# Ten steps of block 2's modulation a layer move from block 1's MLP to its attention

## The chip, the core and the metric

The kernel runs on one core of one Trainium2 chip. A core has five engines, each with its own queue of instructions, worked off in order: PE (TensorE, matrix products), DVE (VectorE) and ACT (ScalarE) for elementwise work, POOL (GpSimd), and SP (SyncE), which here only issues DMA transfers. The engines wait for one another through semaphores. The metric is the device time of one execution in microseconds (us); the profile and the trace come from one such execution, in which a hardware profiler took down each instruction's start and duration. In the rows PE is TensorE's matmuls and PEld its loads of the stationary operand; L12 is line 12 of the kernel.

## The reference, cut to what matters

Two blocks of two layers each, on 256 tokens of width 1024, in float32. Block 1's layer is attention of three kinds, then attention to a memory, then an MLP; each is followed by a layer norm. Block 2's layer needs the vector `mod`, which depends on the input `c` alone, and so can be worked out at any time before.

```python
def first_block(x, mem, ...):
    for l in range(DEPTH):                                   # DEPTH = 2
        y = hybrid_mixer(x, w_in[l], ..., w_gate[l], w_br_nsa[l], w_br_mla[l], w_br_fox[l], w_mix_out[l])
        x = layer_norm(DN_ALPHA * x + y, ln_g[l, 0], ln_b[l, 0])
        y = memory_cross_attention(x, mem, xa_w_q[l], xa_w_kv[l], xa_w_o[l])
        x = layer_norm(DN_ALPHA * x + y, ln_g[l, 1], ln_b[l, 1])
        y = jnp.square(jax.nn.relu(x @ mlp_w_up[l])) @ mlp_w_down[l]     # 1024 x 4096, 4096 x 1024
        x = layer_norm(DN_ALPHA * x + y, ln_g[l, 2], ln_b[l, 2])
    return x

def hybrid_layer(x, c_act, ...):                             # block 2, c_act = silu(c)
    mod = c_act @ w_ada + b_ada                              # w_ada is 1024 x 3072
    shift, scale, gate = jnp.split(mod[:, None, :], 3, axis=-1)
    h = rms_norm_2(x, norm_g) * (1.0 + scale) + shift
    ...
    return x + gate * (merged @ w_out)
```

## The kernel before

Every matrix product is made of three: each float32 operand is split in a rounded part hi and a rest lo, and `mm3` (L138 to L140) issues hi x hi, hi x lo and lo x hi. Weights come in pieces of 128 x 1024 numbers (512 KB). `raw_load` has SP fetch one into the tile `raw` (L76, four buffers); ACT casts it to `hi` (L112), DVE subtracts to get `lo` (L113); `hi` and `lo` have six buffers each. So a buffer of `raw` comes free when DVE has made `lo`, and only then can SP issue the next load: SP's queue is worked off in order, and a load that waits for a buffer holds up those behind it.

**The modulation.** `mod` of a layer is made by 24 steps (`ada_steps`). Each loads 512 KB of `w_ada` into a buffer of `raw` and has DVE multiply it with the conditioning vector and sum along each row (L1641: one instruction of 128 x 1024 and a short one that reads the sum). Neither ACT nor PE takes part. The first step of a layer also loads `c` into `raw`, takes its Tanh on ACT (L1637) and makes silu's double on DVE (L1638) into a tile of the tag `gt`. The steps stand in the list `fillers`, and `fill(n)` runs the next n of it.

**Where they run.** The MLP of block 1 calls `fill`. `up(g)` makes a quarter of the hidden layer: 8 pieces of `w_up`, four PSUM banks `s` one after the other, each cleared by ACT's Relu (L921) and Square (L925), POOL's square (L926) and DVE's difference (L927); behind each bank of `up(1)` to `up(3)` stands a `fill(1)`, twelve in a layer. `down(g)` takes 8 pieces of `w_down`, in two halves; behind each half of `down(0)` and `down(1)` stands a `fill(2)`, and of `down(2)` a `fill(4)`, sixteen in a layer. The order is up 0, up 1, down 0, up 2, down 1, up 3, down 2, down 3. In layer 0 the list begins with `clear_scratch` (POOL clears a tile of the tag `flat` and writes it to two scratch arrays in DRAM, L1660), in layer 1 with the three steps of `trig_steps`.

**What sets the order.** A scheduler orders ACT, DVE, POOL and SP by data, buffers and priorities; in the attention of block 1 PE's order is written by hand (`manual_schedule`): 22 slots, each a piece of two attention jobs, and behind each slot a piece of the dense products (`w_in`'s last parts, then the gates, `w_gate`). The scores of a head block are read by DVE (L275), exponentiated by ACT (L279), scaled by DVE (L286, L288, L290), transposed by PE (L302) and copied from PSUM by ACT (L313) or DVE (L315) in turn. The one bank `t` serves these transposes and those of the compressed attention (L627), so L627 must wait until L315 has copied the bank. L677 takes the copied scores to the values. After the attention to the memory the normalized tokens are transposed by PE (L357) and cast by ACT and DVE (L127, L128); beside that `up_by_token` has made the first 512 hidden features by token (L894 Relu, L895 square on POOL), and `by_feature` transposes them (L902).

Of the kernel before, what the change touches and what calls it, by code (L numbers as in the profile page):

```python
# [42 lines left out]
def program(ctx: ExitStack, tc: tile.TileContext, T: dict, out: bass.AP):  # L43
# [21 lines left out]
    def bt(tag, shape, dt=F32, bufs=1):  # L65
        p = com if tag in COMMON else blk[0]
        return p.tile(shape, dt, tag=tag, name=nm(tag), bufs={**COMMON, "dg": 2, "TT": 2, "Tn": 2}.get(tag, bufs))
# [126 lines left out]
    fillers = []  # L194
# [200 lines left out]
    def block1_layer(l, x, xop, us, K):  # L395
# [10 lines left out]
        if not K:  # L406
            r = [flat2(bt("P", [128, 4, 256], F32, 4)) for g in range(2)]
            w, (h, lo) = raw_tile(), slots()
            for k in range(2):
                x_tiles(0, r[0], k, k + 1)  # L410
                c = slice(512 * k, 512 * k + 512)
# [28 lines left out]
        for j in range(0, 4, 2):  # L440
            p = pst("mm")
# [14 lines left out]
        pool.memset(rep, 0.0)  # L456

        def compress_hidden(i):
            fl = bt("flat", [128, 16, 2, 16])
            pool.memset(fl[:, :, :, 15:16], 0.0)  # L460
            for g in range(2):
                for par in range(2):
                    a = kvT[64 * g:64 * g + 64, i, :]
                    srcv = bass.AP(tensor=a.tensor, offset=a.offset + par,
                                   ap=[list(a.ap[0]), [2, 16], [16, 15]])
                    ver.tensor_add(out=fl[64 * par:64 * par + 64, :, g, 0:15], in0=srcv,
                                   in1=pe_c[64 * g:64 * g + 64, i, par, :].unsqueeze(2).broadcast_to([64, 16, 15]))
            hp = pst("t")
            for kt in range(16):
                q = 32 * (kt % 4)  # L470
                pe.matmul(hp[q:q + 32, :128], lhsT=fl[:, kt].rearrange("p g c -> p (g c)"),
                          rhs=cw1[i][kt // 8][:, 128 * (kt % 8):128 * (kt % 8) + 128], start=kt < 4, stop=kt > 11)
            hq = flat2(bt("PT", [128, 4, 128], F32, 4))[:, 0:128]
            act.copy(out=hq, in_=hp[:, :128])
            hp = pst("t")
            pe.matmul(hp[:, :32], lhsT=hq, rhs=fold4, start=True, stop=True)
            hx = st("hx", [128, 32])
            act.copy(out=hx, in_=hp[:, :32])
            u = st("hu", [128, 32])
            ver.tensor_mul(out=u, in0=hx, in1=hx)  # L480
            ver.tensor_scalar(out=u, in0=u, scalar1=0.044715, scalar2=1.0, op0=ALU.mult, op1=ALU.add)
            ver.tensor_mul(out=u, in0=u, in1=hx)
            act.activation(out=u, in_=u, func=AF.Tanh, scale=math.sqrt(2.0 / math.pi))
            ver.scalar_tensor_tensor(out=hx, in0=u, scalar=1.0, in1=hx, op0=ALU.add, op1=ALU.mult)
            return hx
# [26 lines left out]
        for t in range(2):  # L512
            p = pst("s")
# [210 lines left out]
        with tc.manual_schedule(engines={mybir.EngineType.PE}):  # L724
            if first:
                turn()
            job = {"m": attend_mla, "f": attend_fox, "c": attend_compressed}
            jobs = {}
            pieces = dense()
            for slot in ("m0", "c0", "m1", "m0 c0", "m0 00", "m1 c1", "m1 01", "00 c1", "00 f0", "01 10", "01 10", "f0",  # L730
                         "f0 f1", "10", "10", "10 11", "11", "f1", "f1", "11", "11", "11"):
                for n in slot.split():
                    if n not in jobs:
                        jobs[n] = job[n[0]](int(n[1])) if n[0] in job else attend_nsa(int(n[0]), int(n[1]))
                    next(jobs[n], None)
                next(pieces, None)
            for _ in pieces:
                pass
        x = xs[0]
# [194 lines left out]
        def down(g, op):  # L934
            for c in range(2):
                us = [unit(T["w_down"][l, 16 * c + 4 * g + i]) for i in range(4)]
                gemm_a([ys[0][c], ys[1][c]], op, us, first=g == 0, last=g == 3, t_outer=g == 3 and c == 1)
                if g < 3:
                    fill(2 if g < 2 else 4)
                    continue  # L940
                if c == 1:
                    nrm.params(l, 2)
                    if l + 1 < L:
                        after.extend(unit(T["w_in"][l + 1, 4 + i]) for i in range(4))
                    else:
                        after.append(unit(T["w_wlal"][0], 128, 8))
                        after.append(unit(T["w_in2"][0, 0], 256, 4, pool))
                for t in range(2):
                    nrm.add(t, c, ys[t][c])
                    if c == 1:  # L950
                        nrm.finish(t)
# [662 lines left out]
    def finish(x, r):  # L1614

        fg = aux(T["final_g"].partition_broadcast(128))
        for i in range(2):
            for t in range(2):
# [6 lines left out]
                                         op0=ALU.mult, op1=ALU.mult)  # L1625
                fetch(out[128 * t:128 * t + 128, s], o)

    def ada_steps(l):

        box = {}  # L1630

        def step(j, i):
            def f():
                if not box:
                    r = raw_load(T["c"].partition_broadcast(128))
                    c = box["c"] = bt("gt", [128, 1024])
                    act.activation(out=c, in_=r, func=AF.Tanh, scale=0.5)  # L1637
                    ver.scalar_tensor_tensor(out=c, in0=c, scalar=1.0, in1=r, op0=ALU.add, op1=ALU.mult)  # L1638
                r = raw_load(T["w_ada"][l, j, i])
                o = 8 * j + i  # L1640
                ver.tensor_tensor_reduce(out=r, in0=r, in1=box["c"], scale=1.0, scalar=0.0, op0=ALU.mult,  # L1641
                                         op1=ALU.add, accum_out=mods[l][:, o:o + 1])
                if i == 7:
                    m = mods[l][:, 8 * j:8 * j + 8]
                    ver.scalar_tensor_tensor(out=m, in0=m, scalar=0.5, in1=pv2[l][:, 8 * j:8 * j + 8],
                                             op0=ALU.mult, op1=ALU.add)
                    if j == 1:
                        ver.scalar_tensor_tensor(out=m, in0=m, scalar=1.0, in1=pv2[l][:, 24:32],
                                                 op0=ALU.add, op1=ALU.mult)
            return f  # L1650

        return [step(j, i) for j in range(3) for i in range(8)]
# [1 line left out]
    scratch = {n: dr.tile([128 * 2080], F32, name=n) for n in ("zd", "lt")}  # L1654

    def clear_scratch():
        z = bt("flat", [128, 16, 2, 16]).rearrange("p a b c -> p (a b c)")[:, 0:416]
        pool.memset(z, 0.0)
        for d in scratch.values():
            pool.dma_start(out=flat(d, 0, [2080, 128], [416, 5], [1, 416]),  # L1660
                           in_=z.unsqueeze(1).broadcast_to([128, 5, 416]))
# [45 lines left out]
    with tc.tile_pool(name="b1", bufs=1) as b1, tc.tile_pool(name="s1", bufs=3) as s1:  # L1707
        blk[:] = b1, s1
        xop = new_op(8)
        for l in range(L):  # L1710
            fillers.extend((trig_steps() if l == 1 else [clear_scratch]) + ada_steps(l))
            x, xop, us = block1_layer(l, x, xop, us, K1)
    r = xop
    fill(99)
# [189 lines left out]
```

## Time and profile before

| | |
|---|---|
| median of 3 runs | 1619.14 us (1618.19 to 1619.34) |
| profiled execution | 1620.32 us, of it span 1618.5 us |
| mean granted clock of TensorE over the span | 0.978 of 2.4 GHz |
| PE busy in the span | 1554.8 us, 96% |
| DVE busy | 1100.4 us, 68% |
| ACT busy | 744.8 us, 46% |
| POOL busy | 261.1 us, 16% |

The span runs from the first to the last instruction; what the execution's time has beside it (1.8 us) lies around that. In the trace layer 0 of block 1 has its attention at about 70 to 200 us and its MLP at 290 to 475 us, layer 1 at about 520 to 650 and 745 to 930 us; block 2 follows. A row of the timeline is an instruction's start and duration, its engine and line, the tile it writes and those it reads, and in square brackets how long the engine had been idle before it and whose work ended that.

### The profile page before, as it was taken

How to read it: one execution, taken by the hardware profiler on the slowest of the kernel's cores; microseconds unless marked ns; L12 is line 12 of the kernel's file. 1: busy time of each engine (PE TensorE's matmuls, PEld its weight loads, DVE VectorE, ACT ScalarE, POOL GpSimd, SP SyncE). 2: the span in 40 equal slices, each digit the busy share in tenths (PEclk: the TensorE clock that was granted, in tenths of full speed). 3: DMA queues.
4: the chain of work that ended last, by engine and by line, in shares of the span. 5: the costliest groups of instructions: out<-in, count | busy, mean ns of one | idle time of the engine just before them, and what ended most of it. 6: DMA issues, size and time to landing. Idle time of an engine off the chain costs nothing. (4 is left out here: it accounts for less than half of the span.)

```text
span 1618.5 us, 29835 instructions
## 1 busy us (share of the span) xinstructions
PE 1554.8 (96%) x12106; PEld 1432.2 (88%) x12106; DVE 1100.4 (68%) x1785; ACT 744.8 (46%) x1196; POOL 261.1 (16%) x255
## 2 busy tenths in 40 slices
PE   7999999999999999999999899899999998999998
PEld 6789997999878899988988788899999987999997
DVE  5576568767676766689776787666466775764754
ACT  4665444544445664455543374433444643333441
POOL 1000110101100001201111142401111433201202
PEclk9899999999999999999999989999999999999999
DMA  8733475587776234664777744543355435442451
GB/s 296 257 105 119 158 231 172 179 287 264 266 258 204 89 108 154 204 208 141 253 270 252 265 140 161 162 147 120 102 183 161 155 113 168 163 134 90 154 184 67
DMA packets 81033, 288.98 MB, mean 179 GB/s; under 512 B 9224, under 2 KB 10304, under 8 KB 80896
## 3 DMA queue, kind: packets, MB, share of 16 engines
q1 hardware_dynamic: 78768, 280.07, 51.9%
q0 software_dynamic: 2128, 7.01, 1.5%
q8 instruction: 95, 1.56, 0.4%
q14 instruction: 42, 0.34, 0.1%
HBM read 281.48 MB, written 5.55 MB: 177 GB/s over the span
## 5 line engine op out<-in xcount | busy, mean ns | idle before, releaser
L113 DVE TENSOR_TENSOR lo<-raw,hi 128x1024 fp32r<-128x1024 f32 (+1 forms) x429 | 543.3, 1275 | 227.3 <-ACT hi L112 224.6
L112 ACT CAST hi<-raw 128x1024 fp32r<-128x1024 f32 (+1 forms) x435 | 452.7, 1048 | 508.8 <-PE mm L139 220.9
L138 PE MATMUL mm<-act,hi 128*128 128x256 f32 x1744 | 506.1, 290 | 7.8 <-ACT hi L112 5.8
L140 PE MATMUL mm<-act,lo 128*128 128x256 f32 x1744 | 497.7, 285 | 3.2 <-DVE lo L113 3.2
L139 PE MATMUL mm<-act,hi 128*128 128x256 f32 x1744 | 497.0, 285 | 0.5 <-DVE act L128 0.5
L138 PEld LDWEIGHTS mm<-act,hi 128*128 128x128 f32 x1744 | 336.8, 193 | 15.8 <-ACT hi L112 6.2
L140 PEld LDWEIGHTS mm<-act,lo 128*128 128x128 f32 x1744 | 336.4, 193 | 5.4 <-DVE lo L113 3.9
L139 PEld LDWEIGHTS mm<-act,hi 128*128 128x128 f32 x1744 | 336.6, 193 | 2.0 <-DVE act L128 0.9
L138 PE MATMUL s<-act,hi 128*128 128x256 f32 x448 | 128.5, 287 | 5.5 <-ACT PT L921 5.5
L138 PE MATMUL mm<-hi,act 128*128 128x512 f32 (+1 forms) x320 | 125.2, 392 | 6.5 <-ACT hi L127 5.5
L140 PE MATMUL s<-act,lo 128*128 128x256 f32 x448 | 128.2, 286 | 0.0
L139 PE MATMUL s<-act,hi 128*128 128x256 f32 x448 | 128.2, 286 | 0.0
L139 PE MATMUL mm<-lo,act 128*128 128x512 f32 (+1 forms) x320 | 123.4, 386 | 0.9 <-DVE lo L113 0.9
L140 PE MATMUL mm<-hi,act 128*128 128x512 f32 (+1 forms) x320 | 123.2, 385 | 0.0
L138 PEld LDWEIGHTS s<-act,hi 128*128 128x128 f32 x448 | 87.4, 195 | 6.4 <-ACT PT L921 6.1
L139 PEld LDWEIGHTS s<-act,hi 128*128 128x128 f32 x448 | 87.3, 195 | 0.2
L140 PEld LDWEIGHTS s<-act,lo 128*128 128x128 f32 x448 | 87.5, 195 | 0.0
L1641 DVE CUSTOM_DVE_ANT_0 raw<-raw,gt 128x1024 f32<-128x1024 f32 x48 | 59.5, 1239 | 30.6 <-DMA raw<-in_w_ada 30.3
L138 PEld LDWEIGHTS mm<-hi,act 128*128 128x128 f32 x320 | 61.1, 191 | 19.6 <-ACT hi L127 5.5
L926 POOL TENSOR_TENSOR PT<-PT 128x512 f32<-128x512 f32 x28 | 38.5, 1376 | 236.3 <-ACT act L925 128.4
L138 PE MATMUL mm<-hi,P 128*128 128x512 f32 x192 | 74.8, 389 | 0.0
L139 PE MATMUL mm<-lo,P 128*128 128x512 f32 x192 | 74.8, 389 | 0.0
(519 smaller groups left out, 2439.8 us busy)
## 6 DMA issues: line engine op xcount, KB each, us to landing
raw<-in_w_in SPq DMA_DIRECT2D x119, 512.0 KB, 4.4
raw<-in_w_up SPq DMA_DIRECT2D x64, 512.0 KB, 4.5
raw<-in_w_down SPq DMA_DIRECT2D x64, 512.0 KB, 4.7
raw<-in_w_gate SPq DMA_DIRECT2D x48, 512.0 KB, 3.4
raw<-in_w_ada SPq DMA_DIRECT2D x48, 512.0 KB, 4.5
raw<-in_w_gl SPq DMA_DIRECT2D x48, 512.0 KB, 3.8
raw<-in_w_branch SPq DMA_DIRECT2D x24, 512.0 KB, 3.4
raw<-in_w_br SPq DMA_DIRECT2D x16, 512.0 KB, 3.3
```

The lines of the kernel that those rows point to most:

```text
L112: act.copy(out=h[:, :cols], in_=r[:, :cols])
L113: (eng or ver).tensor_sub(out=l[:, :cols], in0=r[:, :cols], in1=h.bitcast(F32)[:, :cols])
L138: pe.matmul(o, lhsT=lh, rhs=rh, start=first, stop=False)
L139: pe.matmul(o, lhsT=lh, rhs=rl, start=False, stop=False)
L140: pe.matmul(o, lhsT=ll, rhs=rh, start=False, stop=last)
L926: pool.tensor_mul(out=r, in0=r, in1=r)
L1641: ver.tensor_tensor_reduce(out=r, in0=r, in1=box["c"], scale=1.0, scalar=0.0, op0=ALU.mult, op1=ALU.add, accum_out=mods[l][:, o:o + 1])
```

## The change

Nine steps of each layer (the count stops at 20, and 18 of the 22 slots have more than three jobs begun, of which every odd one counts) are run in the attention, by a `fill(1)` behind a slot. What is left of the list runs in the MLP as before, with a `fill(1)` behind each half of `down(0)` to `down(2)`: six there instead of sixteen. `clear_scratch` and `trig_steps` come behind the tenth step. `c` is loaded once, in layer 0's attention, and its product stays in a tile of its own, `cmod`, for both layers; the tiles `flat` become tiles of the tag `mv`.

```diff
         def compress_hidden(i):
-            fl = bt("flat", [128, 16, 2, 16])
+            fl = bt("mv", [128, 16, 2, 16])
...
             pieces = dense()
+            beside = 0
             for slot in ("m0", "c0", "m1", "m0 c0", "m0 00", "m1 c1", "m1 01", "00 c1", "00 f0", "01 10", "01 10", "f0",
                          "f0 f1", "10", "10", "10 11", "11", "f1", "f1", "11", "11", "11"):
                 for n in slot.split():
...
                     next(jobs[n], None)
                 next(pieces, None)
+                if len(jobs) > 3:
+                    beside += 1
+                    if beside % 2 and beside < 20:
+                        fill(1)
...
                 if g < 3:
-                    fill(2 if g < 2 else 4)
+                    fill(1)
                     continue
...
+    box = {}
+
     def ada_steps(l):
 
-        box = {}
 
         def step(j, i):
             def f():
                 if not box:
                     r = raw_load(T["c"].partition_broadcast(128))
-                    c = box["c"] = bt("gt", [128, 1024])
+                    c = box["c"] = bt("cmod", [128, 1024])
                     act.activation(out=c, in_=r, func=AF.Tanh, scale=0.5)
                     ver.scalar_tensor_tensor(out=c, in0=c, scalar=1.0, in1=r, op0=ALU.add, op1=ALU.mult)
                 r = raw_load(T["w_ada"][l, j, i])
...
     def clear_scratch():
-        z = bt("flat", [128, 16, 2, 16]).rearrange("p a b c -> p (a b c)")[:, 0:416]
+        z = bt("mv", [128, 16, 2, 16]).rearrange("p a b c -> p (a b c)")[:, 0:416]
...
         for l in range(L):
-            fillers.extend((trig_steps() if l == 1 else [clear_scratch]) + ada_steps(l))
+            steps = ada_steps(l)
+            fillers.extend(steps[:10] + (trig_steps() if l == 1 else [clear_scratch]) + steps[10:])
             x, xop, us = block1_layer(l, x, xop, us, K1)
```

In the changed kernel the lines behind the slots stand five or six lower: L1641 is L1647 there, L902 is L907. A number behind a tile's name tells one tile of that tag from the next.

SP's queue in layer 0's attention, before, from the last pieces of `w_in` (into `raw`) to the second four of `w_gate`; `xr` takes the tokens:

```order
L76 DMA raw_921<-in_w_in 128x1024
L76 DMA xr_1171<-in_x 128x1024
L76 DMA xr_1173<-in_x 128x1024
L76 DMA raw_1176<-in_w_gate 128x1024
L76 DMA raw_1182<-in_w_gate 128x1024
L76 DMA raw_1188<-in_w_gate 128x1024
L76 DMA raw_1194<-in_w_gate 128x1024
L76 DMA raw_1401<-in_w_gate 128x1024
L76 DMA raw_1407<-in_w_gate 128x1024
```

The same place of the change:

```order
L76 DMA raw_921<-in_w_in 128x1024
L76 DMA raw_954<-in_c 128x1024
L76 DMA raw_959<-in_w_ada 128x1024
L76 DMA raw_1093<-in_w_ada 128x1024
L76 DMA xr_1182<-in_x 128x1024
L76 DMA xr_1184<-in_x 128x1024
L76 DMA raw_1187<-in_w_gate 128x1024
L76 DMA raw_1193<-in_w_gate 128x1024
L76 DMA raw_1199<-in_w_gate 128x1024
L76 DMA raw_1205<-in_w_gate 128x1024
L76 DMA raw_1236<-in_w_ada 128x1024
L76 DMA raw_1355<-in_w_ada 128x1024
```

`c` and two pieces of `w_ada` now stand ahead of the tokens and the gates, and two more between each four pieces of `w_gate`, in the same four buffers.

DVE in layer 0's attention, before, about the copy of bank `t` (L315) for which the second L627 waits:

```order
L275 ISA nmx_1031 128x1
L286 RECIPROCAL sc_1225<-sums_1028 128x4
L288 TENSOR_TENSOR sc_1225<-sc_1225,gate_631 128x4
L290 TENSOR_TENSOR P_1026<-P_1026,sc_1225 128x4x128
L716 COPY fkT_700<-mm_1058 64x256 x2
L315 COPY PT_1098<-t_1093 128x512
L286 RECIPROCAL sc_1229<-sums_1029 128x4
L288 TENSOR_TENSOR sc_1229<-sc_1229,gate_631 128x4
L290 TENSOR_TENSOR P_1027<-P_1027,sc_1229 128x4x128
L113 TENSOR_TENSOR lo_1404<-raw_1401,hi_1403 128x1024
```

In the change two steps (L1647) stand in DVE's queue ahead of this place:

```order
L286 RECIPROCAL sc_1096<-sums_873 128x4
L1647 ISA raw_1236,mod_76<-raw_1236,cmod_956 128x1024
L1647 ISA mod_76 128x1
L315 COPY PT_970<-t_965 128x512
L613 TENSOR_TENSOR pcs_979<-s_980,bias_c 128x4x2x16
L288 TENSOR_TENSOR sc_1096<-sc_1096,gate_631 128x4
L286 RECIPROCAL sc_1100<-sums_874 128x4
L616 TENSOR_REDUCE cm_986<-pcs_979 128x8
L290 TENSOR_TENSOR P_871<-P_871,sc_1096 128x4x128
L617 TENSOR_TENSOR pcs_979<-pcs_979,cm_986 128x128
L288 TENSOR_TENSOR sc_1100<-sc_1100,gate_631 128x4
L1647 ISA raw_1355,mod_76<-raw_1355,cmod_956 128x1024
```

and at the place itself:

```order
L275 ISA nmx_1039 128x1
L113 TENSOR_TENSOR lo_1208<-raw_1205,hi_1207 128x1024
L716 COPY fkT_700<-mm_1066 64x256 x2
L315 COPY PT_1109<-t_1104 128x512
L286 RECIPROCAL sc_1239<-sums_1036 128x4
L286 RECIPROCAL sc_1243<-sums_1037 128x4
L288 TENSOR_TENSOR sc_1239<-sc_1239,gate_631 128x4
L288 TENSOR_TENSOR sc_1243<-sc_1243,gate_631 128x4
L290 TENSOR_TENSOR P_1034<-P_1034,sc_1239 128x4x128
L290 TENSOR_TENSOR P_1035<-P_1035,sc_1243 128x4x128
```

The three instructions L286, L288 and L290 of the first job, which stood ahead of the L315, now stand behind it.

SP's queue in layer 0's MLP, before, from the first half of `down(0)` to the end of its second:

```order
L76 DMA raw_3657<-in_w_down 128x1024
L76 DMA raw_3663<-in_w_down 128x1024
L76 DMA raw_3717<-in_w_ada 128x1024
L76 DMA raw_3720<-in_w_ada 128x1024
L76 DMA raw_3723<-in_w_down 128x1024
L76 DMA raw_3729<-in_w_down 128x1024
L76 DMA raw_3735<-in_w_down 128x1024
L76 DMA raw_3741<-in_w_down 128x1024
L76 DMA raw_3795<-in_w_ada 128x1024
L76 DMA raw_3798<-in_w_ada 128x1024
```

and in the change:

```order
L76 DMA raw_3685<-in_w_down 128x1024
L76 DMA raw_3691<-in_w_down 128x1024
L76 DMA raw_3745<-in_w_ada 128x1024
L76 DMA raw_3748<-in_w_down 128x1024
L76 DMA raw_3754<-in_w_down 128x1024
L76 DMA raw_3760<-in_w_down 128x1024
L76 DMA raw_3766<-in_w_down 128x1024
L76 DMA raw_3820<-in_w_ada 128x1024
```

One piece of `w_ada` now stands behind four of `w_down`, where two stood; in the `up`s it stays at one for two pieces.

PE at the start of layer 0's MLP, before (L357 transposes tokens, L902 the first hidden features):

```order
L140 MATMUL mm_3157<-hi_2951,act_2923 128x512
L357 MATMUL s_3128<-cpack,xr_1173 128x128 x4
L357 MATMUL s_3135<-cpack,xr_1173 128x128 x4
L138 MATMUL mm_3158<-hi_2933,act_2920 128x512
L139 MATMUL mm_3158<-lo_2934,act_2920 128x512
L902 MATMUL t_3340<-cpack,PT_3207 128x128 x3
L140 MATMUL mm_3158<-hi_2933,act_2921 128x512
```

and in the change:

```order
L140 MATMUL mm_3190<-hi_2984,act_2956 128x512
L357 MATMUL s_3161<-cpack,xr_1184 128x128 x4
L907 MATMUL t_3373<-cpack,PT_3240 128x128 x2
L357 MATMUL s_3168<-cpack,xr_1184 128x128 x4
L138 MATMUL mm_3191<-hi_2966,act_2953 128x512
L139 MATMUL mm_3191<-lo_2967,act_2953 128x512
L907 MATMUL t_3373<-cpack,PT_3240 128x128 x2
```

Two transposes of hidden features, which read what POOL's L895 has written, now stand between the two halves of the tokens' transposes.

## Rows read from the trace of the kernel before

**Rows 1.** Windows: busy us of each engine, granted clock, DMA share, GB/s.

```profile
70.00:180.00 110.00, 107.91 (x910) 98.43 (x909) 70.53 (x192) 66.23 (x168) 3.22 (x6) 1.00 0.37 124
...
300.00:420.00 120.00, 117.61 (x810) 109.88 (x809) 86.00 (x97) 57.64 (x69) 14.69 (x12) 1.00 0.80 271
```

**Rows 2.** Groups by line, 300 to 420 us: busy, mean ns, idle before, releasers.

```profile
L112 ACT CAST hi<-raw 128x1024 fp32r<-128x1024 f32 x42 | 44.0, 1049 | 61.8 <-DMA raw<-in_w_down 24.9 <-DMA raw<-in_w_up 21.6 <-DVE mod L1641 5.1
...
L1641 DVE CUSTOM_DVE_ANT_0 raw<-raw,gt 128x1024 f32<-128x1024 f32 x19 | 24.1, 1267 | 11.7 <-DMA raw<-in_w_ada 11.7
```

**Rows 3.** Timeline of DVE and ACT, 410 to 420 us.

```profile
410.46 1.23 DVE L1641 CUSTOM_DVE_ANT_0 raw<-raw,gt 128x1024 f32<-128x1024 f32 x1 [2.95 <-DMA raw<-in_w_ada]
411.61 0.08 DVE L1641 DVE_READ_ACCUMULATOR2_ANT mod<- 128x1 f32 x1
...
416.48 1.05 ACT L112 CAST hi<-raw 128x1024 fp32r<-128x1024 f32 x1 [5.12 <-DMA raw<-in_w_down]
...
419.26 0.59 ACT L921 ACTIVATE PT<-s 128x512 f32<-128x512 f32 x1
```

**Rows 4.** Timeline of PE: its five waits for pieces in the MLPs.

```profile
419.90 0.39 PE L138 MATMUL s<-act,hi 128*128 128x256 f32 x1 [2.39 <-ACT PT L921]
...
826.84 0.39 PE L138 MATMUL s<-act,hi 128*128 128x256 f32 x1 [1.77 <-ACT PT L921]
...
874.76 0.39 PE L138 MATMUL s<-act,hi 128*128 128x256 f32 x1 [1.37 <-ACT PT L921]
...
902.98 0.51 PE L138 MATMUL mm<-hi,act 128*128 128x512 f32 x1 [0.42 <-ACT hi L112]
904.24 0.50 PE L139 MATMUL mm<-lo,act 128*128 128x512 f32 x1 [0.75 <-DVE lo L113]
```

**Rows 5.** Window behind the first of them.

```profile
421.00:425.00 4.00, 4.00 (x24) 4.00 (x23) 2.23 (x4) 2.51 (x4) 2.01 (x2) 0.57 0.57 198
```

**Rows 6.** The page: the steps, and DMA issues with median us to landing.

```profile
L1641 DVE CUSTOM_DVE_ANT_0 raw<-raw,gt 128x1024 f32<-128x1024 f32 x48 | 59.5, 1239 | 30.6 <-DMA raw<-in_w_ada 30.3
...
raw<-in_w_gate SPq DMA_DIRECT2D x48, 512.0 KB, 3.4
raw<-in_w_ada SPq DMA_DIRECT2D x48, 512.0 KB, 4.5
```

**Rows 7.** The conditioning vector's Tanh: ns min/median/max, first and last start.

```profile
L1637 ACT ACTIVATE gt<-raw x2: 1060/1061/1062, 307.0 to 768.5; 128x1024 f32<-128x1024 f32 x2
```

**Rows 8.** Timeline of DVE and PE about the second L627 of layer 0.

```profile
105.25 0.18 DVE L286 RECIPROCAL sc<-sums 128x4 f32<-128x4 f32 x1 [0.30 <-ACT P L279]
...
106.27 0.85 DVE L716 COPY fkT<-mm 64x256 f32<-64x256 f32 x2
...
107.90 0.33 PE L627 MATMUL t<-cpack,pcs 128*128 128x128 f32 x1 [1.19 <-DVE PT L315]
```

**Rows 9.** Timeline of DVE and PE about the first L677, layer 0.

```profile
128.74 0.69 DVE L315 COPY PT<-t 128x512 f32<-128x512 f32 x1
...
130.34 0.66 PE L677 MATMUL mm<-PT,vv 128*64 128x128 f32 x8
```

**Rows 10.** Timeline at the start of layer 0's MLP, and the window before it.

```profile
286.00:294.00 8.00, 7.79 (x38) 6.02 (x38) 6.80 (x13) 2.80 (x5) 1.96 (x2) 1.00 0.00 0
...
291.46 0.42 PEld L357 LDWEIGHTS s<-cpack,xr 128*128 128x128 f32 x4 [0.16 <-issue]
...
291.88 1.04 POOL L895 TENSOR_TENSOR PT<-PT 128x512 f32<-128x512 f32 x1 [2.11 <-ACT PT L894]
...
292.33 0.50 PE L138 MATMUL mm<-hi,act 128*128 128x512 f32 x1 [0.20 <-ACT act L127]
292.97 0.55 PE L902 MATMUL t<-cpack,PT 128*128 128x128 f32 x3
```

**Rows 11.** A PE wait of block 2, and the window behind it.

```profile
1279.06 0.38 PE L1032 MATMUL o<-dg,ones 128*128 128x128 f32 x1 [1.81 <-DVE dg L1031]
...
1279.00:1283.00 4.00, 3.94 (x33) 3.94 (x34) 4.00 (x10) 1.60 (x3) 0.52 (x1) 1.00 0.74 252
```

## The prediction

> **What bounds the kernel now.** I read first the busy time of each engine by stretch [rows 1]. PE is the bound nearly everywhere: 117.61 of the 120 us in layer 0's MLP, 107.91 of 110 us in its attention. What the change can win is therefore only time in which PE stands idle or runs slowly, and no more than that. The two stretches differ in what lies beside PE. In the MLP the transfers are near their own limit (DMA share 0.80, 271 GB/s); in the attention they are not (0.37, 124 GB/s), and DVE has 39.5 of 110 us free there.
>
> Next the groups by line in the MLP's stretch [rows 2]. ACT made 42 casts and DVE 19 steps in 120 us, so 61 pieces of 512 KB went through the four buffers of `raw`. At 271 GB/s a piece (0.524 MB) takes 1.93 us, so 61 pieces take 118 of the 120 us: PE and the pieces run neck and neck, without slack. The reader is to see in the same rows that ACT waited for pieces of `w_down` and `w_up` (24.9 and 21.6 us). That is no loss yet, since six buffers of `hi` and `lo` lie between ACT and PE; it is one when they run empty.
>
> How they run empty stands in the timeline [rows 3]. DVE comes to a step at 410.46 after waiting 2.95 us for `w_ada`. The pieces behind it in the queue wait for buffers that DVE has yet to free; the next `w_down` is cast only at 416.48, ACT having waited 5.12 us with its Relu queued behind the casts. The Relu that clears PSUM bank `s` runs at 419.26, and PE starts its next bank at 419.90 after 2.39 us of idle time [rows 4].
>
> Then all PE waits in both MLPs that end with ACT's Relu, a cast or a `lo` [rows 4]: 2.39, 1.77, 1.37, 0.42 and 0.75, together **6.70 us**. PE's waits at the layers' last norms end otherwise and are not touched. Behind the first, PE runs at a mean granted clock of 0.57 for 4 us [rows 5], that is mostly at 1.2 instead of 2.4 GHz; the stretch behind the second (827 to 831 us) shows 0.57 too. Each loses 4 x 0.43 = 1.72 us. So the pieces' lateness costs 6.70 + 2 x 1.72 = **10.1 us**.
>
> **The change part by part.**
> *What it removes from the MLPs.* In layer 0's MLP up to 420 us, twenty fillers become sixteen, and the steps 15 instead of 19; 57 pieces at 1.93 us are 110 us, which leaves 10 us of slack in 120 instead of 2. The halves of `down` now carry one piece of `w_ada` for four of `w_down` instead of two; the `up`s stay as they are. A step less also takes 1.24 us off DVE [rows 6], behind which buffers come free. I take all 10.1 us as won. The bounds are half of that, if only the `down`s recover (the first rival), and all of it; nothing else of PE's time there can be won.
>
> *c once instead of twice.* Layer 1 saves a load, a Tanh of 1.06 us [rows 7] and a product on DVE. They lay beside PE's work, at the start of the MLP, while the buffers were full: 0. In layer 0 the same three come at the attention's start. ACT's Tanh there stands ahead of the first job's exponentials; ACT is busy 66.23 of 110 us and DVE 70.53 [rows 1], so both can catch up before PE needs them: 0. Should that cover fail, the Tanh costs its 1.06 us and the product on DVE as much as a step.
>
> *The steps in the attention*, nine a layer. One is 1.15 us from its start to the next instruction (410.46 to 411.61) [rows 3], up to 1.24 + 0.08. Nine are some 11 us, in 39.5 us of DVE's free time: on average they fit, and PE loses only where it already waits for DVE or nearly does. I looked for such places by the slack between a DVE instruction and the PE instruction that reads its result, and found two.
>
> (1) The second L627 waits 1.19 us for DVE's L315, for bank `t` [rows 8]; layer 1's does so too, 1.20 us. In the change, two steps stand ahead of that L315. Against them DVE had 0.30 us free there, and L286 to L290, 1.02 us (105.25 to 106.27), go behind it. Two steps at 1.15 to 1.24 less 1.32 make **+1.1 us** a layer. Bounds: 0, if DVE catches up before; 2.5, if the moved three are not yet ready to give way.
>
> (2) The first L677 starts at 130.34 and reads what L315 leaves at 129.43 [rows 9]: 0.9 us of slack, and DVE may be a step late. I take **+0.3 us** a layer, bounds 0 and 1.5.
>
> In layer 1 two steps also stand ahead of the rotation of a query that PE needs early: +0.1, bounds 0 and 1.2 (one step).
>
> Nine loads of `w_ada` go between those of `w_gate`, through the same four buffers. They are taken at 4.5 us in the MLP, while `w_gate` lands in 3.4 [rows 6], so a gate's piece is at worst some two loads later; the gates' casts wait for buffers of `hi` that PE frees, not for pieces, and hide this: 0. Where they did not, it would be a wait of PE for a cast.
>
> *clear_scratch.* Its clearing and two transfers go to the start of layer 0's MLP, behind the norm, where no transfer runs (DMA share 0.00) [rows 10]: 0. POOL's instructions behind it are the second L895 and its like; if that had to wait for the two transfers, it would cost PE some us once.
>
> *The start of layer 0's MLP.* The order puts two of the L902 between the halves of L357. Before, the second half started loading at 291.46; now it waits for POOL's L895, which ends at 292.92 (291.88 + 1.04) [rows 10]. PE's next product, which started at 292.33, comes 1.5 us later, of which the 0.55 us of L902 are done in the wait: **+1.0 us**, once; bounds 0 and 1.4.
>
> *The sum.* 1620.32 (the profiled execution, 1618.5 of it span) - 10.1 + 2 x (1.1 + 0.3) + 0.1 + 1.0 = 1614.1 us. The profiled execution is 1.2 us above the median of 1619.14, so a measured median of **1613 us**. The measurement can tell about 0.2%, 3.2 us: faster is under 1615.9, slower over 1622.4.
>
> **The rivals.**
> *A. The `up`s stay the bound.* They still carry one step for two pieces of `w_up`, 12 pieces in some 23 us (12 x 1.93), as before, and the first three waits [rows 4] all fall in an `up`. The lead that the `down`s win back may not reach through the next `up`. Half of the 10.1 us then stays: 1614.1 + 5.05 - 1.2 = **1618 us**, the same. Against it: 10 pieces in a `down` leave it 3.9 us ahead, more than the 2.39 us of the longest wait.
>
> *B. The clock falls in the attention.* The second L627 would wait 1.19 + 1.1 = 2.3 us. In this trace the clock fell behind waits of 2.39 and 1.77 us [rows 4, 5], but stayed at 1.00 behind one of 1.81 us [rows 11]. Were it to fall in both layers, by 1.72 us as above, 1613 + 3.4 = **1616.4 us**, the same. The Trainium skill (TensorE: Matmul & The Clock Gate, Part 1) says that the slow clock is PE's default and that only activity keeps it away, so that a wait costs more than its length. Rows 5 agree; rows 11 show a wait that did not. By that rule alone the sum would be the 1616.4 us of this rival; by rows 11 it stays at 1613.
>
> *C. All of it is hidden in the attention.* DVE has caught up at each place, and the start of the MLP costs nothing: 1619.1 - 10.1 = **1609 us**.
>
> *D. Slower: DVE waits for `w_ada` in the attention.* DVE takes its queue in order. A step whose piece has not landed holds back the copies of PSUM behind it, for which PE waits. Over the 48 steps before, DVE waited 30.3 us for `w_ada` [rows 6], 0.63 us a step. Were 18 steps to bring that to PE, 18 x 0.63 = 11.4 us on top of the 3.9 us of the sum: 1612.9 + 11.4 = **1624 us**. It is slower than before from (1622.4 - 1612.9) / 18 = 0.53 us a step. Against it: the attention's transfers are at 0.37 and land faster, the loads of a pair are issued well ahead of their steps, and PE has slack against DVE nearly everywhere.
>
> That the steps do not move at all is excluded by the order.
>
> **How the numbers follow.** The forecast (1610.5 to 1615.9 us) 0.54, C 0.13, A 0.13, B 0.08, D 0.12. Faster is the forecast and C, 0.67; same A and B, 0.21; slower D, 0.12. The predicted time is the forecast's, 1613. The range must leave out no more than 0.2: it takes in C, A and B, with 1608 (C, less the 1 us by which the runs before lie apart) to 1620 (A, with place 2 at its upper bound in both layers, 2 x 1.2 more), and leaves out D.
>
> **What the profile of the changed kernel would show.** Right: no PE wait for ACT's Relu over 0.5 us in the two MLPs, a granted clock of 1.00 at the stretches of rows 5, ACT's waits for `w_down` in the MLP well below 24.9 us; L627's wait at about 2.3 us in both layers; the L895 wait at the MLP's start. DVE busier in the attention by some 11 us of 110, and DMA share there up from 0.37 to about 0.50 (9 x 0.524 MB in 110 us are 43 GB/s on top of 124). Wrong: the Relu's waits in the `up`s still there (A); a half clock behind L627 (B); DVE idle for `w_ada` in the attention for more than some 0.5 us a step with PE waiting for L315 or L275's successors (D). A wait for a piece of `w_gate` would show that the four buffers are the bound there, which the sum puts at 0.

## The result, and the profile after

The changed kernel takes 1605.71 us (median of 4 runs, 1603.23 to 1607.72), the kernel before 1619.24 us beside it (1618.19 to 1622.14): ratio 0.9919, 95% interval 0.9896 to 0.9942. The interval leaves out 1, so it is faster, as forecast, but by 13.5 us instead of 6, and the time lies under the range. The profiled execution took 1603.23 us, its span 1601.5 us.

First the waits that the forecast was about. Windows of the changed kernel (busy us of PE, PEld, DVE, ACT, POOL, then granted clock, DMA share, GB/s): layer 0's attention and MLP, and the 4 us where the first long waits of the MLPs had been followed by a slow clock.

```profile
69.00:179.00 110.00, 106.65 (x899) 97.06 (x898) 80.35 (x211) 65.86 (x168) 3.24 (x6) 1.00 0.50 168
...
298.00:418.00 120.00, 120.00 (x824) 112.15 (x823) 82.67 (x92) 60.36 (x71) 15.93 (x13) 1.00 0.78 262
417.00:421.00 4.00, 4.00 (x35) 4.00 (x35) 3.05 (x3) 3.23 (x4) 0.64 (x2) 1.00 0.83 282
...
819.00:823.00 4.00, 4.00 (x36) 4.00 (x35) 2.06 (x4) 3.23 (x4) 0.91 (x2) 1.00 0.74 259
```

PE is now busy for all 120 us of the MLP's stretch (117.61 in [rows 1]), and the clock stays at 1.00 where it was 0.57 [rows 5]. All five waits of [rows 4] are gone. DVE has 10 us more to do in the attention, and DMA share there went from 0.37 to 0.50, as worked out.

The groups of the MLP's stretch, 298 to 418 us, answer to [rows 2]:

```profile
L112 ACT CAST hi<-raw 128x1024 fp32r<-128x1024 f32 x44 | 46.2, 1050 | 57.9 <-DMA raw<-in_w_up 17.6 <-DMA raw<-in_w_down 16.2 <-PE s L139 9.9
...
L1647 DVE CUSTOM_DVE_ANT_0 raw<-raw,cmod 128x1024 f32<-128x1024 f32 x15 | 19.2, 1278 | 15.6 <-DMA raw<-in_w_ada 15.4
```

Fifteen steps instead of 19, as counted. ACT still waits 16.2 us for `w_down` (24.9 before), but now also for PE (9.9 us): the buffers of `hi` are full at times, so the casts have a lead.

PE's waits at the places where a cost was expected, in this order: the second L627 of layer 0 and of layer 1, the first L677, the L907 at the MLP's start.

```profile
107.05 0.33 PE L627 MATMUL t<-cpack,pcs 128*128 128x128 f32 x1 [1.33 <-DVE PT L315]
...
555.98 0.33 PE L627 MATMUL t<-cpack,pcs 128*128 128x128 f32 x1 [1.33 <-DVE PT L315]
...
130.68 0.55 PE L677 MATMUL mm<-PT,vv 128*64 128x128 f32 x6 [1.12 <-DVE PT L315]
...
293.21 0.33 PE L907 MATMUL t<-cpack,PT 128*128 128x128 f32 x1 [1.43 <-POOL PT L900]
```

L627 waits 0.13 us longer, not 1.1 [rows 8]. L677 waits 1.12 us where it had not waited [rows 9], in layer 0 only. L907 waits for POOL as forecast [rows 10].

**Where the time went.** The matmuls come in nearly the same order in both kernels, so the starts of the same matmul in the two traces can be subtracted. The table gives how much this difference changes within a stretch, in us, for the first profile of each kernel (places by the times of the kernel before; a minus is time won). A slow clock is a stretch with a granted clock of half the full one, 1.2 instead of 2.4 GHz.

| stretch | us | what stands there |
|---|---|---|
| 0 to 60 | -1.0 | a slow clock of 6.8 instead of 10.2 us; nothing changed there but clear_scratch, which ran at 42 us before and runs at 284 us after |
| 60 to 285, attention 0 | +1.3 | L677 +1.06, L627 +0.13 |
| 285 to 300 | +1.0 | L907 |
| 300 to 480, MLP 0 | -4.2 | the wait at 419.90 and the clock behind it |
| 480 to 740, attention 1 | -1.5 | a slow clock at 527 us that is not there after; L627 +0.12 |
| 740 to 915, MLP 1 | -6.8 | -3.5 (wait at 826.84 and clock), -1.6, -1.7 |
| 915 to 945, last norm | -2.8 | the wait of 1.84 us at 927.90, and a slow clock of 6.8 instead of 10.2 us behind it |
| block 2 | -3.1 | unchanged code |

What the change did between these two profiles is 1.3 + 1.0 - 4.2 - 6.8 - 2.8 = **-11.5 us**. The other 5.6 us of the span's 17 are slow clock at places that the change does not touch; the experiments show that they come and go. The size depends on which execution of the kernel before is taken: against its second profile (below) the same sum is about -13.5 us, since that one waits longer in the MLPs.

The forecast put the last norm at nothing. In the kernel before, ACT's casts for the last half of `down(3)` and for the first pieces of block 2 wait for pieces:

```profile
912.02 1.05 ACT L112 CAST hi<-raw 128x1024 fp32r<-128x1024 f32 x1 [1.38 <-DMA raw<-in_w_down]
915.36 1.05 ACT L112 CAST hi<-raw 128x1024 fp32r<-128x1024 f32 x1 [2.29 <-DMA raw<-in_w_down]
919.32 1.05 ACT L112 CAST hi<-raw 128x1024 fp32r<-128x1024 f32 x1 [2.91 <-DMA raw<-in_w_wlal]
```

DVE's queue there, before: the `lo` of the last of these stands ahead of the norm's additions (L334), and PE's transposes (L357) wait for the norm.

```profile
920.40 1.23 DVE L113 TENSOR_TENSOR lo<-raw,hi 128x1024 fp32r<-128x1024 f32 x1 [2.74 <-ACT hi L112]
921.55 1.28 DVE L334 SCALAR_TENSOR_TENSOR xr<-xr,mm 128x512 f32<-128x512 f32 x2
...
927.90 1.29 PE L357 MATMUL s<-cpack,xr 128*128 128x128 f32 x8 [1.84 <-DVE xr L350]
```

After the change the last such `lo` starts at 902.33, the additions follow at 903.48, 11 us ahead of the transposes at 914.65, and DVE then waits for PE:

```profile
902.33 1.23 DVE L113 TENSOR_TENSOR lo<-raw,hi 128x1024 fp32r<-128x1024 f32 x1 [1.50 <-ACT hi L112]
903.48 1.28 DVE L334 SCALAR_TENSOR_TENSOR xr<-xr,mm 128x512 f32<-128x512 f32 x2
...
909.41 0.69 DVE L334 SCALAR_TENSOR_TENSOR xr<-xr,mm 128x512 f32<-128x512 f32 x1 [3.46 <-PE mm L140]
```

### The profile page after: what moved, and what is told of

It is laid out like the page before. It is cut to its first block, busy times and chain, and to the rows that moved or that the text cites. A ratio compares the mean times of both kernels' runs of the same rounds, so it can differ in the third digit from the quotient of the medians.

```text
span 1601.5 us, 29832 instructions
## 1 busy us (share of the span) xinstructions
PE 1545.1 (96%) x12106; PEld 1425.9 (89%) x12106; DVE 1094.9 (68%) x1784; ACT 741.1 (46%) x1193; POOL 255.9 (16%) x255
## 4 chain that ended last, share of the span: by engine, by line
PE 79%; DVE 10%; ACT 3%; DMA 3%; issue 3%; POOL 2%; SPq 0%; DVEq 0%; POOLq 0%; ACTq 0%
PE mm L138 19%; PE mm L140 18%; PE mm L139 18%; PE s L140 3%; PE s L139 3%; PE s L138 3%; DVE lo L113 3%; ACT hi L112 2%; PE s L270 1%; DMA raw<-in_w_in 1%; PE o L657 1%; DMA zd<-PT 1%; PE s L1173 1%; PE o L1275 1%; PE t L1275 1%
## 5 line engine op out<-in xcount | busy, mean ns | idle before, releaser
L1647 DVE CUSTOM_DVE_ANT_0 raw<-raw,cmod 128x1024 f32<-128x1024 f32 x48 | 62.0, 1292 | 39.0 <-DMA raw<-in_w_ada 38.7
L138 PE MATMUL mm<-hi,P 128*128 128x512 f32 x192 | 74.8, 389 | 0.0
L140 PE MATMUL mm<-hi,P 128*128 128x512 f32 x192 | 74.7, 389 | 0.0
```

What stands on the lines that cost most here:

```text
L138: pe.matmul(o, lhsT=lh, rhs=rh, start=first, stop=False)
L140: pe.matmul(o, lhsT=ll, rhs=rh, start=False, stop=last)
```

## The experiments

Theory 1: the gain is that of the pieces that no longer go through the MLPs' four buffers. Times are beside runs of the kernel before on the same chip; ratios are against it, with 95% intervals. "By the rows" means the starts of the same matmuls, subtracted as in the table.

**Both kernels again** (no edit).

> The kernel before, unchanged, for a second profile. Theory 1 (pieces): the five waits for pieces in the MLPs (2.39, 1.77, 1.37, 0.42, 0.75 us) and the 1.84 us wait for the last norm come back within 0.5 us each, time about 1619 us. The slow-clock stretches behind the same unchanged waits of block 2 (44 us of half clock before, 34 us after the change) come out otherwise than in the first profile. Rival (block 2 is slowed for a reason that the change removes): block 2 shows the same slow stretches as in the first profile, at about 44 us.

> The changed kernel, unchanged, for a second profile and a narrower time. Theory 1: about 1605.5 us; none of the MLP waits for pieces; waits in front of L677 (1.12 us, layer 0) and of L907 (1.43 us) come back; block 2's slow-clock stretches differ from those of the first profile by some us. Rival: block 2's slow stretches are again about 34 us long, at the same places.

> The changed kernel once more, beside e_five_clear on one chip. Theory 1: block 1 ends as in its two other profiles (the same waits, within 1 us apart from slow-clock stretches before 80 and at 525 us); block 2, unchanged code, differs by up to 4 us. Rival (block 2 is really faster after the change): it takes 3 us less than in the kernel before again.

The kernel before against itself: 1.0002 (0.9985 to 1.0018). Its waits came back as 2.31, 2.63 and 0.74 us and 1.70 before layer 1's last norm, but not the ones at 875 and 903 us: which waits come varies by execution. Layer 0's last norm was late too this time, with `lo` halves ahead of it in DVE's queue; the second row is the same place after the change.

```profile
473.92 1.29 PE L357 MATMUL s<-cpack,xr 128*128 128x128 f32 x8 [1.86 <-DVE xr L350]
```

```profile
468.81 1.29 PE L357 MATMUL s<-cpack,xr 128*128 128x128 f32 x8 [0.85 <-DVE xr L350]
```

The changed kernel: 1604.02 us, 0.9921 (0.9898 to 0.9944), and 1607.72 us, 0.9936 (0.9917 to 0.9956), with the same waits in its three profiles and none for pieces in the MLPs. Against the first profile of before all three win 4.2 us in layer 0's MLP, 6.8 in layer 1's and 2.8 to 3.2 at the last norm. Single runs spread widely: 1608 to 1620 us for the kernel before in 23 runs, 1599 to 1613 for the changed one. Block 2 (from its first matmul to the end), windows of before, before again, and the changed kernel's three profiles:

```profile
934.78:1618.55 683.77, 653.58 (x5784) 622.69 (x5784) 440.02 (x715) 280.11 (x415) 159.31 (x159) 0.97 0.44 142
```

```profile
935.78:1617.54 681.76, 655.17 (x5784) 623.87 (x5784) 440.32 (x715) 280.09 (x415) 158.73 (x159) 0.97 0.43 143
```

```profile
921.31:1601.46 680.15, 651.08 (x5784) 620.46 (x5784) 440.71 (x715) 280.26 (x415) 157.19 (x159) 0.97 0.44 143
```

```profile
923.48:1603.05 679.57, 650.41 (x5784) 619.59 (x5784) 440.44 (x715) 280.16 (x415) 157.76 (x159) 0.98 0.43 143
```

```profile
925.32:1610.96 685.64, 657.72 (x5784) 625.60 (x5784) 440.68 (x715) 280.45 (x415) 158.41 (x159) 0.96 0.44 142
```

The same 5784 matmuls took 680.2, 679.6 and 685.6 us after the change, at a mean clock of 0.97, 0.98 and 0.96. So the 3 us of block 2 in the first profile are no effect of the change: the rival, that block 2 is faster after it, falls. Block 2 begins at 934.8 and 935.8 before, at 921.3, 923.5 and 925.3 after: 12 us earlier in the mean.

**The small parts alone**: in the changed kernel all steps go back to the MLP.

```diff
-                if len(jobs) > 3:
...
-                    fill(1)
+                    fill(2 if g < 2 else 4)
```

> The small parts alone: c loaded once and kept in its own tile, the tile tag merged, clear_scratch and trig_steps behind the tenth step, but all steps in the MLP as before. Theory 1 (the gain is that of fewer pieces in the MLP): the five waits for pieces stay, no gain: 1619 us, up to 1.5 us more for the wait at the start of the MLP, whose order changes as in the change. Rival (the small parts carry a good part of the gain): 1612 us or less.

Measured 0.9996 (0.9977 to 1.0016). The interval shows no gain, but the profile shows what neither theory expected: layer 0 has its wait of 2.42 us,

```profile
423.51 0.39 PE L138 MATMUL s<-act,hi 128*128 128x256 f32 x1 [2.42 <-ACT PT L922]
```

and layer 1's MLP has none left, though all 24 steps are in it. That is 6.4 us less in that stretch than in the first profile of before, with 1.0 us more for L907; the last norm still waits 1.38 us. A steady gain of the 5 us that this leaves would lie outside the interval of the ten executions, so this one profile does not stand for all of them.

**The place of trig_steps.**

```diff
-            fillers.extend(steps[:10] + (trig_steps() if l == 1 else [clear_scratch]) + steps[10:])
+            fillers.extend((trig_steps() if l == 1 else [clear_scratch]) + steps)
```

on top of the last edit.

> As e_c_once, but clear_scratch and trig_steps stand first in the list again, so only c's single load and the tile tags differ from the kernel before. Theory 1b (in layer 1 it was the place of trig_steps that took the waits away): the waits at 827, 875 and 904 us and the 1.8 us one before the last norm come back, time as before within 2 us. Rival (c's second load): layer 1 stays free of them, some 7 us under the kernel before in the profile.

Measured 1.0009 (0.9990 to 1.0027), and in layer 1 two waits for pieces in the MLP (3.10 and 0.56 us) and the one before the last norm are back, though not the one at 875:

```profile
827.77 0.58 PE L138 MATMUL s<-act,hi 128*128 128x256 f32 x1 [3.10 <-ACT PT L922]
...
927.00 0.44 PE L357 MATMUL s<-cpack,xr 128*128 128x128 f32 x1 [2.70 <-DVE xr L350]
```

So c's second load is not what counts: it is left out here too. What is left between the two kernels is the place: with it, the first ten steps run while the casts still have a lead, and three fillers without a load stand in the middle. That the place takes layer 1's waits away rests on one profile of each; the two times do not show it.

**No steps at all.** All 48 are left out, and c's load and the `fill` in the attention with them.

```diff
-            fillers.extend(steps[:10] + (trig_steps() if l == 1 else [clear_scratch]) + steps[10:])
+            fillers.extend(trig_steps() if l == 1 else [clear_scratch])
```

> All 48 steps and the load of c are left out (the modulation is then zero), everything else as in the change. Theory 1: no waits for pieces in the MLP, as after the change, and no cost in the attention either: the wait in front of L677 goes (1.06 us), those of L627 are 1.2 us, so 1 to 2.5 us under the changed kernel, 1603 to 1604.5 us. Rival (the remaining fifteen steps a layer still slow the MLP): 1600 us or less, with the difference in the MLPs.

Measured 1601.68 us, 0.9916 (0.9886 to 0.9947). The attention's stretch, 60 to 285 us, is within 0.3 us of the kernel before; the L677 wait is gone and L627 waits 1.19. The MLPs win 4.2 and 6.9 us by the rows, as much as in the change (4.2 and 6.8): the fifteen steps left cost PE nothing there.

**Loads with a sixteenth of DVE's product, and the product without loads**, in the kernel before. The second also makes `flat` a tile of the tag `mv`, as the change does.

```diff
-                ver.tensor_tensor_reduce(out=r, in0=r, in1=box["c"], ...
+                ver.tensor_tensor_reduce(out=r[:, :64], in0=r[:, :64], in1=box["c"][:, :64], ...
```

```diff
-                r = raw_load(T["w_ada"][l, j, i])
+                r = bt("junk", [128, 1024])
...
-                ver.tensor_tensor_reduce(out=r, in0=r, in1=box["c"], scale=1.0, ...
+                ver.tensor_tensor_reduce(out=r, in0=box["c"], in1=box["c"], scale=1e-4, ...
```

> The kernel before, but each step's product on DVE takes 64 columns instead of 1024 (the modulation is then wrong): all loads stay, in the same order, and 1.2 us of DVE a step goes to some 0.2. Theory 1 (the pieces' transfers and buffers make the lateness): the waits in the MLPs stay for the most part, 1 to 4 us faster at most. Rival (DVE's time makes it: buffers of raw come free late because DVE is busy): the waits go, 9 to 13 us faster.

> The kernel before, but the steps load nothing: DVE's product reads the conditioning vector twice, at the same size, into a tile of its own (the modulation is then wrong; flat is merged into mv to make room). Theory 1: the waits in both MLPs go, 10 to 13 us faster. Rival (DVE's time): they stay, 3 us faster at most.

Measured 0.9931 (0.9904 to 0.9957) and 0.9952 (0.9937 to 0.9967). Both take all of PE's waits for pieces in the MLPs away and win there, by the rows, 4.2 and 6.8 or 6.9 us, as the change does. So the transfers alone are not the cause, as theory 1 had it for the first of these runs, and DVE's time alone, its rival, is not either. The window of e_load_only, 300 to 420 us:

```profile
300.00:420.00 120.00, 120.00 (x832) 112.47 (x831) 67.23 (x103) 60.57 (x72) 15.30 (x13) 1.00 0.83 280
```

All loads are there, at 280 GB/s instead of 271, and PE does not wait. What remains is that a piece holds one of four buffers for all of its way: transfer, wait for its engine, and its time on DVE. Taking away most of the side pieces' time on DVE was enough, and so was taking them out of the buffers.

The second run also shows where the wait at L907 comes from (L902 in its numbering):

```profile
293.84 0.44 PE L902 MATMUL t<-cpack,PT 128*128 128x128 f32 x2 [1.43 <-POOL PT L895]
```

It is there with clear_scratch first in the list, in this run as in e_c_trig_first, and not in e_load_only, which keeps `flat`. With the tag merged and clear_scratch in the MLP's part of the list, its clearing runs at 282 to 287 us instead of 42, and the order of L357 and the hidden features' transposes changes. So the 1.0 us belong to the merged tag, not to the steps.

**Three buffers** in the changed kernel.

```diff
-        return wp.tile([128, 1024], F32, tag="raw", name=nm("raw"), bufs=4)
+        return wp.tile([128, 1024], F32, tag="raw", name=nm("raw"), bufs=3)
```

> The changed kernel with three buffers of raw instead of four. Theory 1 in the form that the two runs without loads and without DVE's product leave (each piece holds one of four buffers for its transfer, its wait and its work on DVE, and it is these together that limit the pieces): a buffer less takes a quarter of the rate, the waits in the MLPs come back, more of them than before the change, and the time is above that of the kernel before. Rival (the path of the transfers is the limit): three transfers under way fill it as well as four, and the MLPs stay as in the change.

Measured 1645.64 us, 1.0181 (1.0158 to 1.0205). Its window of 300 to 420 us, and two of PE's waits:

```profile
300.00:420.00 120.00, 117.11 (x780) 108.73 (x779) 73.62 (x81) 54.62 (x64) 13.41 (x11) 0.99 0.72 233
```

```profile
373.54 0.54 PE L138 MATMUL s<-act,hi 128*128 128x256 f32 x1 [2.58 <-ACT PT L926]
...
423.71 0.39 PE L138 MATMUL s<-act,hi 128*128 128x256 f32 x1 [3.02 <-ACT PT L926]
```

The transfers fall to 233 GB/s at a DMA share of 0.72: here it is the buffers that limit them, not the path. The waits are back from 373 us on, 46 us ahead of the first one before the change. Not all of the loss lies in the MLPs: by the rows against the kernel before, the stretches of the two attentions lose 5.9 and 10.3 us, those of the MLPs 5.9 and 3.6.

**Five and eighteen steps** a layer in the attention.

```diff
-                    if beside % 2 and beside < 20:
+                    if beside % 4 == 1 and beside < 20:
...
-                    fill(1)
+                    fill(1 if g < 2 else 3)
```

```diff
-                    if beside % 2 and beside < 20:
+                    if beside < 20:
```

> Five steps a layer in the attention; the halves of down(0) and down(1) take one step, those of down(2) three. Theory 1 (a threshold: waits come only where the pieces' lead is used up): layer 1 is free of waits, as with no step in the attention once trig_steps stand behind the tenth step; layer 0 is free up to 420 us, and the three steps behind each half of down(2) cost little, as PE's last halves have a lead again. As the changed kernel within 2 us. Rival (gain in proportion to the steps moved): half of the changed kernel's gain, 5 us slower than it.

> Eighteen steps a layer in the attention instead of nine (a step behind each slot with more than three jobs begun). Theory 1: the MLPs have no wait left to lose already with nine, so they gain nothing more; DVE in the attention takes 9 x 1.2 = 11 us more a layer, and PE's waits for copies there grow: 1 to 5 us slower than the changed kernel. Rival D of the prediction (DVE waits for w_ada in the attention and PE for DVE): 8 us slower than the changed kernel or more.

Five: 0.9944 (0.9922 to 0.9966). There is no wait for pieces in the MLPs, which win 4.2 and 6.8 us by the rows, as with nine: the gain is a threshold, not a proportion. The time alone could not tell, since half the gain lies in its interval too. There is no wait at L677, and L627 waits 0.86 us, less than before. Eighteen: 0.9923 (0.9895 to 0.9951); the time is as with nine, within its interval. The stretch of 60 to 285 us, less the clock at 75 us, costs 3.8 instead of 1.3 us: L677 waits 1.25, and a later wait of 1.85 us at 272 has a slow clock behind it. Against that, clear_scratch runs in the attention here and L907 does not wait. Rival D's 8 us are not there.

**clear_scratch first again**, and the same with five steps.

```diff
-            fillers.extend(steps[:10] + (trig_steps() if l == 1 else [clear_scratch]) + steps[10:])
+            fillers.extend(([clear_scratch] if l == 0 else []) + steps[:10] + (trig_steps() if l == 1 else []) + steps[10:])
```

> The changed kernel with clear_scratch first in layer 0's list again; the second half of L357 then stands ahead of L907 again, as before the change. Theory 1: the 1.43 us wait in front of L907 goes, 1.0 us under the changed kernel; eight steps instead of nine in layer 0's attention bring no wait back in the MLP. Rival (the wait only moves on, to L907 itself or the cast behind it): the same time as the changed kernel.

> Five steps a layer in the attention, as in e_dose5, with clear_scratch first in the list again, as in e_clear_first (so four steps and it in layer 0's attention). Theory 1: neither the wait in front of L677 (1.1 us) nor the one in front of L907 (1.4 us) is there, no wait for pieces in the MLPs; 2 to 2.5 us under the changed kernel in the stretch up to the end of block 1, the times of block 2 apart by up to 4 us either way. Rival (the steps left in layer 0's MLP, 20, bring a wait back): a wait before 480 us, no gain over the changed kernel.

With nine: the wait at L907 is gone and 285 to 300 us takes as long as before the change. The time is nevertheless 0.9951 (0.9936 to 0.9966); in its profile block 2 takes 685.9 us against 680.2 in the first of the changed kernel, with a clock of 0.965 against 0.974. The gain of 1.0 us is shown by the rows, not by the time. With five: 1602.51 us, **0.9910** (0.9895 to 0.9924), beside 1607.72 us and 0.9936 of the changed kernel on the same chip. No wait at L677 or L907, block 2 begins at 918.8 us, the earliest of the kernels that do all the work. The medians lie 5 us apart, of which the rows explain 2.5; the intervals overlap.

## Why the prediction was right or wrong

**The bound and the MLPs: right.** Twenty fillers became sixteen, the five waits went, and the clock with them. The term was 10.1 us; the starts of the same matmuls say 11.0 (4.2 + 6.8). It was under-sized because it added the waits, not what the starts of the matmuls lost at them, 7.6 us for 6.7.

**"PE's waits at the layers' last norms end otherwise and are not touched": wrong**, and the step that failed most. The row of 927.90 names DVE's norm as what PE waited for; ahead of the norm in the same queue stood the `lo` halves, late for the same pieces. The term was put at nothing and measured 2.8 us in layer 1; the wait is gone in every run that takes the pieces' waits away in both layers, but for 0.57 us in e_load_only. In the second profile of before layer 0's last norm adds 1.0 us (a wait of 1.86 against 0.85).

**The attention: too dear.** L627 was put at +1.1 a layer and is +0.13. The working set the two steps against the 0.30 us that DVE had free at that place alone; in the 32 us ahead of it (75 to 107 us) DVE had been busy for 24.8, and the steps fitted in what was free. L677 was put at +0.3 a layer and is +1.06 in layer 0, nothing in layer 1. In layer 0, DVE waits 2.01 us for `w_ada` at 118.36 with a copy behind it; in layer 1 it waits 0.38 at the same place.

```profile
118.36 1.23 DVE L1647 CUSTOM_DVE_ANT_0 raw<-raw,cmod 128x1024 f32<-128x1024 f32 x1 [2.01 <-DMA raw<-in_w_ada]
...
119.51 0.69 DVE L315 COPY PT<-t 128x512 f32<-128x512 f32 x1
```

That is rival D's mechanism, once, at a price of 1 us. With five steps, where this step does not stand there, the copy that L677 reads starts 1.82 us behind PE's transposes (L302) instead of 3.85, and L677 does not wait. That the wait for `w_ada`, and not the step's own 1.15 us, makes the difference is not shown. Sum: 1.3 + 0.1 against 2.9.

**The MLP's start: right**, +1.0 at L907, and taken away where clear_scratch runs in the attention. The forecast ascribed it to the order alone; what changed the order was the tile tag.

**The rivals.** A fell: the lead reached through the `up`s. B fell with its premise, since L627's wait grew to 1.33, not 2.3 us. C's 1609 us was nearer than the forecast, but not by its mechanism: it had no cost in the attention and at the MLP's start, where the rows show 2.4 us, and no gain at the last norm. D stayed at one place.

**The reason given for the MLPs was wrong in one point.** The rate of 1.93 us a piece was read as the transfers' limit; it was only what the four buffers let through (280 GB/s in e_load_only, 233 with three buffers). In layer 1 the place of trig_steps may be a second sufficient cause of the MLP's gain; the forecast gave it no price, and one profile each is all that speaks for it.

With the terms as they measured, the sum is 1619.2 - 11.5 = 1607.7 us, at the edge of the range, or about 1605.7 us with the 13.5 us against the second profile of before. The corrected mechanism thus reaches the measured time, but which of the two sums holds for the median is open: single executions move by some 6 us either way, and on other chips the changed kernel's medians were 1604.02 and 1607.72 us, 10 to 12 us under the kernel before beside them. That the time fell 2.3 us outside the range is in part chance.

## What to carry to other kernels

Side work with its own loads belongs where the load buffers and the engine that frees them have slack; five steps a layer moved were enough here; nine and eighteen won no more in the MLPs and cost more in the attention. When pieces run late, look beyond PE's waits for pieces: whatever stands behind them in the same engine's queue is late too, as the last norm was. A tile tag that is merged in passing can move other work: here it took clear_scratch from 42 to 284 us and cost 1.0 us. And a rate that is observed is not a limit: leave out one part at a time (load, product, buffer) before calling one.

## What was not expected of the hardware

Single executions of one kernel spread by 12 us (1608.08 to 1620.41 in 23 runs). The same 5784 matmuls of block 2 took 678.2 to 687.7 us over the kernels' profiles, with a mean granted clock of 0.96 to 0.98, while PE's waits there add up to 20 to 23 us in every profile. The wait of 1.81 us [rows 11] was followed by a slow clock within 2 us in four of the fifteen profiles and not in the others. So a gain of 1 us in this kernel is to be read from the rows of its place, not from the time.
